# Up projection of a hybrid decoder layer: ten places for the split weights, and a small fp32 product per segment

## The chip, the core and the metric

The kernel runs on one core of one Trainium2 chip. The metric is the device time of one execution in microseconds; lower is better. The time before is 2170.84 us, the median of two runs (2167.92 and 2173.75).

## What is computed

One layer of a decoder on x of 512 tokens by 2048, in float32. Token mixing (a projection, gated linear attention in four heads, differential attention in four heads, an output projection) is followed by a gated MLP with a causal convolution over time. The change lies in the MLP's first product, `h @ w_ffn_in`:

```python
def conv_ffn(h, w_ffn_in, conv_w, conv_b, w_ffn_out):
    S = h.shape[1]
    up = h @ w_ffn_in
    a, b = up[..., :D_FF], up[..., D_FF:]
    a_pad = jnp.pad(a, ((0, 0), (CONV_W - 1, 0), (0, 0)))
    a = (conv_w[0] * a_pad[:, 0:S] + conv_w[1] * a_pad[:, 1:S + 1]
         + conv_w[2] * a_pad[:, 2:S + 2] + conv_b)
    return (jax.nn.gelu(a, approximate=True) * b) @ w_ffn_out
```

D_FF is 5632, so `w_ffn_in` has 2048 rows and 11264 columns, and `w_ffn_out` 5632 rows and 2048 columns.

## The kernel before

**Precision.** Every large product is made of three fp32r products: each operand is split into a high half (ScalarE rounds it to fp32r, line 135) and a low half (VectorE subtracts, line 136), and high x high, high x low and low x high are added up in PSUM. Products in plain fp32 (the small ones of attention, lines 439, 507, 538) are single calls of `mm`.

**Granules and the ring.** Weights come in granules of 128 x 1024 floats (512 KB). `granule` (line 126) splits one into two slots of a tile named ring, of 7 x 1024 columns (line 108). `halves` (line 111) takes the slots in turn: three for high halves (0, 1, 2) and three for low halves (3, 4, 5). `place_w` shifts every slot by so many columns of four bytes; the shift is the "place". Token operands lie in the tiles ah, al (high and low) and s5, s2, s3. Token operands, weights slots at place 0 and ring all begin at the same offset in a row of 128 columns (512 bytes), so place 16 sets weights 16 columns off the tokens.

**The up projection.** It begins with two pairs of column blocks by the plain scheme (`mm_t`, lines 163 to 173; place 0, lines 171 to 173), of which the first stands in a section whose order is written by hand (`to_ffn`). The other 40 blocks of 128 columns of each branch are made in ten groups `gi` of 4 blocks; each group has two units, one for each branch (`br`): 20 units in `ups` (line 1052). A unit is a Strassen-like scheme: seven segments x0, z0, y0, z1, x1, y1, y2 (lines 876 to 911) in place of eight block products. Each segment takes two granules of 24 matmuls (`up_prods`, lines 916 to 926: 128 x 128 weights, 256 tokens), so a unit has 7 x 2 x 24 = 336 matmuls. The order of segments is y0, z1, x1, y1 of a unit, x0 of the next, y2 of this, z0 of the next (lines 1053 to 1077). Some granules are sums of weight blocks: a DMA of GpSimd adds into the tile (line 873), or VectorE does (lines 889, 907). A unit's chains hold one PSUM bank each of two pools, psm (x and z) and psa (y), with four banks each.

**The down projection** (down units, lines 1015 to 1050, from line 1074 on) uses the same `run`, with 128 x 128 token blocks as weights and 512 columns of granule as the moving operand, at place 0. Its token operands are read back from DRAM and split (`prepare`, line 1010, with `split`, lines 147 to 149). The first down unit's x0 stands between y1 and y2 of the last up unit.

**What sets the order.** Outside the hand-written sections a scheduler orders each engine's instructions by a simulated timeline: an instruction that depends on nothing goes where the engine would otherwise wait. ScalarE, VectorE and TensorE then run their own lists in order, and semaphores carry the dependencies, those of overlapping columns of the ring among them.

Of the kernel before, what the change touches and what calls it, by code (L numbers as in the profile page):

```python
# [35 lines left out]
def hybrid_layer(ctx: ExitStack, tc: tile.TileContext, x, attn_pre_norm, w_in, w_alpha_up, b_alpha,  # L36
# [19 lines left out]
    mm = nc.tensor.matmul  # L56
# [5 lines left out]
    psa = ctx.enter_context(tc.tile_pool(name="psa", bufs=4, space=PSUM))  # L62


    ident = few.tile([P, P], F32, name="ident")
    make_identity(nc, ident)
    nhalf = few.tile([P, 4], F32, name="nhalf")
# [9 lines left out]
    def bank(pool=None):  # L77
        return (pool or psa).tile([P, 512], F32, name="bank", tag="bank")
# [27 lines left out]
    place_w = [0]  # L106
# [19 lines left out]
    def granule(src, a, raw=None, spare=None, hl=None):  # L126
        if raw is None:
            raw = load(src, a)
        if hl is not None:
            hi, lo = hl[:, 0, :], hl[:, 1, :]  # L130
        elif spare:
            hi, lo = spare_halves(spare)
        else:
            hi, lo = halves()
        act(hi, raw, AF.Copy)  # L135
        tt(lo, raw, hi.bitcast(F32), ALU.subtract)  # L136
        r = "p (a b) -> p a b"
        return hi.rearrange(r, a=a), lo.rearrange(r, a=a)
# [8 lines left out]
    def split(hi, lo, src):  # L147
        act(hi, src, AF.Copy)  # L148
        tt(lo, src, hi.bitcast(F32), ALU.subtract)  # L149
# [615 lines left out]
    def pair_tile():  # L765
        return small_tile("u").rearrange("p (n t) -> p n t", n=2)


    def conv(c, b, f):
        act(c, b, AF.Identity, bias=conv_col(3, f), scale=conv_col(2, f))  # L770
        stt(c[:, 1:], b[:, :S - 1], conv_col(1, f), c[:, 1:], ALU.mult, ALU.add)
        stt(c[:, 2:], b[:, :S - 2], conv_col(0, f), c[:, 2:], ALU.mult, ALU.add)
        act(c, c, AF.Gelu_apprx_tanh)
# [82 lines left out]
    class Unit:  # L856
# [4 lines left out]
        def run(self, seg, op, raws):  # L861
            c = seg[0]
            if seg[1] == "0":
                self.banks[c] = self.chain(c)
            for g in range(2):
                turn[0] += 1
                place_w[0] = 16 if self.a == 4 else 0
                hl = granule(None, self.a, raws[g], spare=extra[0] and turn[0] % 4 == 0)
                self.prods(self.banks[c], op, g, hl, seg[1] == "0")

# [42 lines left out]
    NOW = dict(skip_group_check=True)  # L913
# [16 lines left out]
    def up_unit(gi, br):  # L930
        col0 = DFF * br + 512 * gi
        T = [slice(0, 256), slice(256, 512)]
        st = {}

        def block(i, j, g):
            return w_f3[:, HK * i + 4 * g:HK * i + 4 * g + 4, col0 + 256 * j:col0 + 256 * (j + 1)]

        def chain(c):
            return bank(psa if c == "y" else psm)

        def out(seg, b):
            v = b.rearrange("p (n t) -> p n t", n=2)
            if seg == "x0":
                st["p1"] = fp.tile([P, 2, 256], F32, name="p1", tag="p1", bufs=2)
                act(st["p1"], v, AF.Copy)
            elif seg == "z0":
                st["u1"] = pair_tile()
                tt(st["u1"][:, :, T[1]], v, st["p1"], ALU.subtract)
            elif seg == "y0":
                stt(st["u1"][:, :, T[0]], v, -1.0, st["p1"], ALU.mult, ALU.subtract)  # L950
            elif seg == "z1":
                tt(st["u1"][:, :, T[0]], st["u1"][:, :, T[0]], v, ALU.add)
            elif seg == "x1":
                st["u0"] = pair_tile()
                act(st["u0"][:, :, T[0]], v, AF.Copy)
            elif seg == "y1":
                tt(st["u1"][:, :, T[1]], st["u1"][:, :, T[1]], v, ALU.subtract)
                if br == 0:
                    activate(1)
                else:  # L960
                    product(1)
            elif seg == "y2":
                tt(st["u0"][:, :, T[1]], v, st["p1"], ALU.add)
                if br == 0:
                    activate(0)
                else:
                    product(0)
                    token_sums(gi, st["u0"], st["u1"])

        def activate(j):  # L970
            c = held[gi, j] = pair_tile()
            for n in range(2):
                conv(c[:, n, :], st[f"u{j}"][:, n, :], 4 * gi + 2 * j + n)

        def product(j):
            u = st[f"u{j}"]
            tt(u, u, held.pop((gi, j)), ALU.mult)

        return Unit(4, block, up_prods, chain, out)


    def token_sums(gi, u0, u1):
        c, i = (gi - 1) // 2, (gi - 1) % 2
        T = [slice(0, 256), slice(256, 512)]
        a11, a21, a12, a22 = u0[:, :, T[0]], u0[:, :, T[1]], u1[:, :, T[0]], u1[:, :, T[1]]

        def put(n, src):
            dma(sd[c][n][:, i, :].rearrange("p (n t) -> p n t", n=2), src)

        def add(n, x, y, op):  # L990
            t = fp.tile([P, 2, 256], F32, name=n, tag="sum", bufs=2)
            tt(t, x, y, op)
            put(n, t)
            return t

        put("a11", a11)
        put("a12", a12)
        put("a22", a22)
        s5 = add("s5", a21, a22, ALU.subtract)
        s2 = add("s2", s5, a11, ALU.subtract)  # L1000
        add("s7", a11, a21, ALU.subtract)
        add("s3", s2, a12, ALU.add)
# [7 lines left out]
    def prepare(c, n):  # L1010
        raw = small_tile("st")
        dma(raw, sd[c][n].rearrange("p g x -> p (g x)"))
        split(piece(ah, *place[n]), piece(al, *place[n]), raw)
# [17 lines left out]
    def down_unit(c, cb):  # L1031
        def block(i, j, g):
            gi = 2 * c + 1 + g
            col = 1024 * cb + 512 * j
            return w_y3[:, 4 * gi + 2 * i:4 * gi + 2 * i + 2, col:col + 512]

        def chain(ch):
            return [bank(psm if ch == "x" else psa) for _ in range(2)]

        def out(seg, b):  # L1040
            for j in range(2):
                if seg == "x0":
                    into(accp[j][:, 512 * cb:512 * (cb + 1)], b[j], 1, c == 0)
                    continue
                half, col, sign = {"z0": (1, 1, 1), "y0": (0, 1, -1), "z1": (0, 1, 1), "x1": (0, 0, 1),
                                   "y1": (1, 1, -1), "y2": (1, 0, 1)}[seg]
                sl = slice(1024 * cb + 512 * col, 1024 * cb + 512 * (col + 1))
                into(acc[2 * half + j][:, sl], b[j], sign, c == 0 and seg in ("z0", "y0", "x1", "y2"))

        return Unit(2, block, down_prods, chain, out)  # L1050

    ups = [up_unit(gi, br) for gi in range(1, NG) for br in range(2)]
    for i, u in enumerate(ups):
        nxt = ups[i + 1] if i + 1 < len(ups) else None
        if i == 0:
            u.x0()
            u.z0()
        u.y0()
        u.z1()
        if i == 0:  # L1060
            for h, r in enumerate(s7raw):
                split(up["s7"][0][:, h], up["s7"][1][:, h], r)
        if nxt is None:
            prepare(0, "a11")
        u.x1()
        if nxt is None:
            prepare(0, "s5")
        u.y1()
        if nxt is not None:
            nxt.x0()  # L1070
            u.y2()
            nxt.z0()
        else:
            downs = [down_unit(c, cb) for c in range(NG // 2) for cb in range(2)]
            downs[0].x0()
            prepare(0, "s2")
            u.y2()
# [163 lines left out]
```

## Time and profile before

| what | us |
|---|---|
| median of two runs | 2170.84 |
| profiled execution: span from first to last instruction | 2150.8 |
| median less span | 20.0 |
| matmuls busy | 2112.4 |
| weight loads busy | 1875.4 |
| VectorE busy | 1414.6 |
| ScalarE busy | 898.3 |
| up projection in units, first to last matmul of lines 924 to 926 | 928 to 1705 |

The profile gives no device time of the profiled execution beside its span; it is set beside the median of the two runs. PE stands for matmuls and PEld for weight loads; both are issued by TensorE and overlap. A group's row names line, engine, operation, out<-in, shape and count, then busy us and mean ns of one, then idle time of the engine ahead of it and who ended it. In a timeline each row has start in us, length in us, engine, line and operation; in brackets the idle time before it and who ended that. Lengths of matmuls reach past the start of the next, so the pace of a stream is read from starts.

### The profile page before, as it was taken

How to read it: one execution, taken by the hardware profiler on the slowest of the kernel's cores; microseconds unless marked ns; L12 is line 12 of the kernel's file. 1: busy time of each engine (PE TensorE's matmuls, PEld its weight loads, DVE VectorE, ACT ScalarE, POOL GpSimd, SP SyncE). 2: the span in 40 equal slices, each digit the busy share in tenths (PEclk: the TensorE clock that was granted, in tenths of full speed). 3: DMA queues.
4: the chain of work that ended last, by engine and by line, in shares of the span. 5: the costliest groups of instructions: out<-in, count | busy, mean ns of one | idle time of the engine just before them, and what ended most of it. 6: DMA issues, size and time to landing. Idle time of an engine off the chain costs nothing.

```text
span 2150.8 us, 31861 instructions
## 1 busy us (share of the span) xinstructions
PE 2112.4 (98%) x13009; PEld 1875.4 (87%) x13009; DVE 1414.6 (66%) x1725; ACT 898.3 (42%) x1162; POOL 199.2 (9%) x242
## 2 busy tenths in 40 slices
PE   7999999999999999999999999999999899999998
PEld 6878888888888889999999999999999778787786
DVE  5345554443444237688777786777778777888887
ACT  4233332333343224344544553544454554443433
POOL 1000000000000001011111111111110111110100
PEclk9999999999999999999999999999999999999999
DMA  6322222223224335455776757667577777676653
GB/s 214 99 75 79 79 69 79 79 79 88 78 80 169 95 128 186 128 119 136 172 172 149 175 139 189 149 157 191 129 172 177 203 229 182 171 195 170 158 167 145
DMA packets 218471, 303.83 MB, mean 141 GB/s; under 512 B 11776, under 2 KB 155572, under 8 KB 216404
## 3 DMA queue, kind: packets, MB, share of 16 engines
q1 hardware_dynamic: 165204, 238.87, 33.4%
q0 software_dynamic: 53120, 62.92, 19.1%
q8 instruction: 102, 1.67, 0.3%
q14 instruction: 45, 0.37, 0.1%
HBM read 273.97 MB, written 27.79 MB: 140 GB/s over the span
## 4 chain that ended last, share of the span: by engine, by line
PE 46%; issue 45%; POOL 4%; DVE 3%; DMA 2%; ACT 1%; POOLq 0%; SPq 0%; DVEq 0%; ACTq 0%
PE bank L189 7%; PE bank L190 7%; PE bank L191 7%; PE bank L173 5%; PE bank L171 5%; PE bank L172 5%; POOL rt L873 2%; PE bank L926 2%; PE bank L925 2%; PE bank L924 2%; POOL raw L873 2%; PE bank L439 1%; PE bank L507 1%; PE bank L538 1%; DVE ring L136 1%
## 5 line engine op out<-in xcount | busy, mean ns | idle before, releaser
L136 DVE TENSOR_TENSOR ring<-raw,ring 128x1024 fp32r<-128x1024 f32 x305 | 371.6, 1221 | 353.8 <-ACT ring L135 344.1
L135 ACT ACTIVATE ring<-raw 128x1024 fp32r<-128x1024 f32 x305 | 323.1, 1060 | 596.6 <-PE bank L191 157.3
L926 PE MATMUL bank<-ah,ring 128*128 128x256 f32 x1280 | 353.7, 276 | 0.8 <-DVE ring L136 0.8
L924 PE MATMUL bank<-ah,ring 128*128 128x256 f32 x1280 | 353.5, 276 | 0.0
L925 PE MATMUL bank<-al,ring 128*128 128x256 f32 x1280 | 353.4, 276 | 0.0
L136 DVE TENSOR_TENSOR ring<-rt,ring 128x1024 fp32r<-128x1024 f32 x221 | 269.0, 1220 | 89.8 <-ACT ring L135 87.9
L135 ACT ACTIVATE ring<-rt 128x1024 fp32r<-128x1024 f32 x221 | 233.1, 1060 | 223.5 <-PE bank L925 146.1
L926 PEld LDWEIGHTS bank<-ah,ring 128*128 128x128 f32 x1280 | 240.3, 188 | 1.2 <-DVE ring L136 1.2
L925 PEld LDWEIGHTS bank<-al,ring 128*128 128x128 f32 x1280 | 240.4, 188 | 0.1
L924 PEld LDWEIGHTS bank<-ah,ring 128*128 128x128 f32 x1280 | 240.3, 188 | 0.1
L189 PE MATMUL bank<-ring,ah 128*128 128x512 f32 x600 | 236.9, 398 | 0.8 <-ACT ah L148 0.8
L190 PE MATMUL bank<-ring,ah 128*128 128x512 f32 x600 | 235.8, 394 | 0.0
L191 PE MATMUL bank<-ring,al 128*128 128x512 f32 x600 | 235.0, 394 | 0.0
L171 PE MATMUL bank<-ah,ring 128*128 128x512 f32 (+1 forms) x512 | 196.2, 383 | 0.0
L173 PE MATMUL bank<-ah,ring 128*128 128x512 f32 (+1 forms) x512 | 194.7, 380 | 0.0
L172 PE MATMUL bank<-al,ring 128*128 128x512 f32 (+1 forms) x512 | 194.5, 380 | 0.0
L1022 PE MATMUL bank<-ring,ah 128*128 128x512 f32 x424 | 166.7, 393 | 7.3 <-DVE ring L136 7.2
L1023 PE MATMUL bank<-ring,al 128*128 128x512 f32 x424 | 165.8, 391 | 0.0
L1021 PE MATMUL bank<-ring,ah 128*128 128x512 f32 x424 | 158.8, 393 | 3.2 <-ACT ring L135 2.4
L191 PEld LDWEIGHTS bank<-ring,al 128*128 128x128 f32 x600 | 113.2, 189 | 24.3 <-DVE al L149 0.3
L189 PEld LDWEIGHTS bank<-ring,ah 128*128 128x128 f32 x600 | 113.1, 189 | 24.2 <-ACT ah L148 1.2
L190 PEld LDWEIGHTS bank<-ring,ah 128*128 128x128 f32 x600 | 113.3, 189 | 23.7 <-DVE ring L136 0.5
(260 smaller groups left out, 4063.6 us busy)
## 6 DMA issues: line engine op xcount, KB each, us to landing
raw<-in_w_in_dram SPq DMA_DIRECT2D x96, 512.0 KB, 3.7
raw<-in_w_ffn_in_dram SPq DMA_DIRECT2D x96, 512.0 KB, 5.1
raw<-in_w_ffn_out_dram SPq DMA_DIRECT2D x48, 512.0 KB, 7.3
rt<-in_w_ffn_in_dram SPq DMA_DIRECT2D x40, 512.0 KB, 6.6
rt<-in_w_ffn_in_dram POOLq DMA_DIRECT2D x40, 512.0 KB, 6.2
raw<-in_w_ffn_in_dram POOLq DMA_DIRECT2D x40, 512.0 KB, 6.8
raw<-in_w_o_dram SPq DMA_DIRECT2D x32, 512.0 KB, 3.7
rt<-in_w_ffn_out_dram SPq DMA_DIRECT2D x20, 512.0 KB, 8.1
```

What stands on the lines that cost most here:

```text
L135: act(hi, raw, AF.Copy)
L136: tt(lo, raw, hi.bitcast(F32), ALU.subtract)
L171: mm(o, wh, ah[:, t0:t1, kk, :], start=st, stop=False)
L172: mm(o, wh, al[:, t0:t1, kk, :], start=False, stop=False)
L173: mm(o, wl, ah[:, t0:t1, kk, :], start=False, stop=sp)
L189: mm(banks[t], ah[:, t, s, :], w[0][:, k, :], start=st, stop=False)
L190: mm(banks[t], ah[:, t, s, :], w[1][:, k, :], start=False, stop=False)
L191: mm(banks[t], al[:, t, s, :], w[0][:, k, :], start=False, stop=sp)
L924: mm(o, wh, sh[:, :, kk, :], start=start and kk == 0 and n == 0, stop=False, **NOW)
L925: mm(o, wh, sl[:, :, kk, :], start=False, stop=False, **NOW)
L926: mm(o, wl, sh[:, :, kk, :], start=False, stop=kk == HK - 1, **NOW)
L1022: mm(b[j], sh[:, o:o + P], w[1][:, q, :], start=False, stop=False, **NOW)
```

## The change

```diff
             for g in range(2):
                 turn[0] += 1
-                place_w[0] = 16 if self.a == 4 else 0
+                place_w[0] = self.place if self.a == 4 else 0
+                if self.a == 4 and g == 0:
+                    mm(nudge[0][:, 0:4], ident, nhalf, start=True, stop=True, **NOW)
                 hl = granule(None, self.a, raws[g], spare=extra[0] and turn[0] % 4 == 0)
                 self.prods(self.banks[c], op, g, hl, seg[1] == "0")
...
+    nudge = [bank(psa)]
     ups = [up_unit(gi, br) for gi in range(1, NG) for br in range(2)]
+    for i, u in enumerate(ups):
+        u.place = (16, 32, 48, 64, 80, 96, 112, 8, 24, 0)[i // 2]
     for i, u in enumerate(ups):
         nxt = ups[i + 1] if i + 1 < len(ups) else None
```

Up units have `self.a == 4`, down units 2. The units of the first group keep place 16; the other nine groups get 32, 48, 64, 80, 96, 112, 8, 24 and 0, one place for each pair of units. Because x0 and z0 of the next unit stand around y2 of this one, the place changes three times where two groups meet. A product in plain fp32 (the identity, 128 x 128, as weights, four columns of -0.5 as the moving operand; line 869 of the changed kernel) is written at the first granule of each segment, 140 in all. It writes a PSUM bank of pool psa that nothing reads. In the changed kernel the lines behind line 866 move by 2, those behind line 1051 by 5.

## The prediction

> **What bounds the kernel now.** I read the page first (shares, then the costliest groups), then busy time by stretches, then the timeline of the stretch that the change touches.
>
> ```profile
> span 2150.8 us, 31861 instructions
> PE 2112.4 (98%) x13009; PEld 1875.4 (87%) x13009; DVE 1414.6 (66%) x1725; ACT 898.3 (42%) x1162; POOL 199.2 (9%) x242
> PEclk9999999999999999999999999999999999999999
> L136 DVE TENSOR_TENSOR ring<-raw,ring 128x1024 fp32r<-128x1024 f32 x305 | 371.6, 1221 | 353.8 <-ACT ring L135 344.1
> L135 ACT ACTIVATE ring<-raw 128x1024 fp32r<-128x1024 f32 x305 | 323.1, 1060 | 596.6 <-PE bank L191 157.3
> ```
>
> TensorE is busy for 98% of the span, so whatever lengthens its stream lengthens the kernel. The diff touches the up projection (matmuls of lines 924 to 926, from 928 to 1705 us). By stretches (columns: stretch, length, busy time and count of PE, PEld, DVE, ACT, POOL, clock, DMA):
>
> ```profile
> core 0: us, PE busy (x) PEld busy (x) DVE busy (x) ACT busy (x) POOL busy (x), PEclk, DMA share, GB/s
> 945.00:1130.00 185.00, 185.00 (x1635) 185.00 (x1634) 140.22 (x144) 89.45 (x99) 25.25 (x20) 1.00 0.70 163
> 1140.00:1340.00 200.00, 200.00 (x1767) 200.00 (x1766) 150.63 (x153) 91.66 (x99) 26.08 (x21) 1.00 0.72 171
> 1366.00:1569.00 203.00, 203.00 (x1793) 203.00 (x1792) 153.99 (x157) 92.53 (x101) 27.99 (x22) 1.00 0.71 167
> 1693.90:1697.00 3.10, 3.10 (x9) 2.45 (x8) 2.33 (x3) 1.18 (x2) 0.86 (x1) 0.51 0.79 159
> ```
>
> In the up projection matmuls and weight loads are both gapless: hundreds of us without a wait. DVE is at 75%, ACT under 50%, DMA at 70%. So the stage's time is the number of matmuls, 20 units of 336 = 6720, times the spacing of their starts. The whole list of waits holds only this for PE there (us in total, times, longest):
>
> ```profile
> PE bank L926 <- DVE ring L136: 1.8, 4, 0.6
> ```
>
> The spacing is not one number. First and last of 25, of 67 and of 64 matmuls, in that order, with the event ahead of them or behind them that matters (fp32 transposes at 837.77, waits at 943.40 and 1134.30):
>
> ```profile
> 837.77 1.15 PE L156 MATMUL bank<-ident,xr 128*128 128x128 f32 x9
> ...
> 839.11 0.28 PE L171 MATMUL bank<-ah,ring 128*128 128x256 f32 x1
> ...
> 841.98 0.28 PE L171 MATMUL bank<-ah,ring 128*128 128x256 f32 x1
> ```
> ```profile
> 928.03 0.28 PE L924 MATMUL bank<-ah,ring 128*128 128x256 f32 x1
> ...
> 935.80 0.28 PE L924 MATMUL bank<-s5h,ring 128*128 128x256 f32 x1
> ...
> 943.40 0.39 PE L926 MATMUL bank<-s2h,ring 128*128 128x256 f32 x1 [0.57 <-DVE ring L136]
> ```
> ```profile
> 1134.30 0.39 PE L926 MATMUL bank<-s2h,ring 128*128 128x256 f32 x1 [0.42 <-DVE ring L136]
> ...
> 1144.73 0.28 PE L924 MATMUL bank<-ah,ring 128*128 128x256 f32 x1
> ...
> 1151.87 0.28 PE L924 MATMUL bank<-ah,ring 128*128 128x256 f32 x1
> ```
>
> Line 171 multiplies the same shape from the ring at place 0: 2.87/24 = 0.120 us. The up projection at place 16 starts at 7.77/66 = 0.118 and later stands at 7.14/63 = 0.1133. So the same instruction has at least three paces; the first is at distance 0, the other two at distance 16. The 0.118 ends at the wait of 943.40 and does not come back: behind the wait of 1134.30 the pace is 0.1133 again.
>
> **The change, part by part.** *The products.* One fp32 product of 4 moving columns for each of 20 x 7 segments: 140. The nearest row is the fp32 product of line 439, 64 columns, which the trace shows as two instructions each (4 heads x 7 levels x 4 products = 112):
>
> ```profile
> L439 PE MATMUL bank<-qe,d 128*128 128x64 f32 x224 | 27.7, 268 | 0.0
> ```
> ```profile
> 160.72 0.39 PE L191 MATMUL bank<-ring,al 128*128 128x512 f32 x1
> 160.94 1.00 PE L439 MATMUL bank<-qe,d 128*128 128x64 f32 x8
> 161.75 0.48 PE L189 MATMUL bank<-ring,ah 128*128 128x512 f32 x1
> 162.07 1.00 PE L439 MATMUL bank<-qe,d 128*128 128x64 f32 x8
> 162.88 0.48 PE L190 MATMUL bank<-ring,ah 128*128 128x512 f32 x1
> 163.19 0.40 PE L191 MATMUL bank<-ring,al 128*128 128x512 f32 x1
> 163.43 0.40 PE L189 MATMUL bank<-ring,ah 128*128 128x512 f32 x1
> ```
>
> From 160.72 to 163.19 are 2.47 us for three 512-column matmuls (0.23 each by their undisturbed starts here, 0.22 to 0.24) and 16 fp32 instructions: 1.78/16 = 0.111 us each. Each instruction comes with a weight load of 128 columns, whatever it streams, so I take 0.111 for 4 columns too: 140 x 2 x 0.111 = **+31 us**. Lower end 0.81/8 = 0.101 from one batch alone (28 us), upper end 0.15 if each also ran dry, a third more than the row (42 us); I stay at the row. They are not at the heads of granules: nothing depends on them, and in the order of the built program they stand in 22 batches (of 1 to 15), all ahead of the middle of the group with place 80, where the scheduler saw PE wait. Four batches of 15 stand where the place goes back (below). The rest may swallow the four waits above: -1 us. Their PSUM bank is one of four of which the stage uses one at a time: nothing.
>
> *The places.* Each place holds for two units, 672 matmuls, so 1 ns of spacing is 0.67 us. Place 16 stays at 0.1133. Place 0 is line 171's case, 0.120: 672 x 6.7 ns = +4.5 us. For 64 the nearest rows are the forget gate's matmuls, whose weight slices are 80 columns wide, so that slice k begins 80k columns on:
>
> ```profile
> 124.77 0.40 PE L386 MATMUL bank<-ah,gas 128*80 128x512 f32 x1
> ...
> 126.60 0.40 PE L386 MATMUL bank<-ah,gas 128*80 128x512 f32 x1
> ...
> 128.44 0.40 PE L386 MATMUL bank<-ah,gas 128*80 128x512 f32 x1
> ```
>
> Of the 8 matmuls in each gap none but these has 0.40, and the pattern returns after 1.83 us, after four slices: 320 columns, 64 beyond two rows of 128. So distance 64 looks like distance 0, and 80 like 16: 64 costs +4.5 us, 80 nothing. For 32, 48, 96, 112, 8 and 24 no row exists; by the three paces they lie between 0.1133 (0) and 0.120 (+4.5 each). I take the middle, 0.1167: 6 x 672 x 3.3 ns = +13.4 us (0 to +27; a gain is not excluded, a 256-column stream could be faster).
>
> The Trainium skill speaks against any effect of distance: "TensorE: Matmul & The Clock Gate", section "Part 2: What happens when you issue a matmul", gives PE two independent SBUF read ports, so that a weight load takes nothing from a running matmul. By it this term would be 0. The trace's paces of 0.120 and 0.1133 for one shape do not agree, unless the way of entering alone makes them.
>
> *The ring where the place changes.* Slots are 1024 columns apart and shift with the place. Where a granule with a lower place follows one with a higher place, its first columns lie on the last ones of the granule just before, and its split must wait until PE is done with that. The kernel before has this once, at its end, where place 16 meets place 0:
>
> ```profile
> 1691.13 1.06 ACT L148 ACTIVATE ah<-st 128x1024 fp32r<-128x1024 f32 x1 [0.26 <-DMA st<-sd0s]
> 1705.81 1.06 ACT L135 ACTIVATE ring<-rt 128x1024 fp32r<-128x1024 f32 x1 [1.77 <-PE bank L925]
> ```
> ```profile
> 1693.33 0.50 PE L1022 MATMUL bank<-ring,ah 128*128 128x512 f32 x1 [4.65 <-DVE ring L136]
> ...
> 1706.92 0.73 PE L1021 MATMUL bank<-ring,ah 128*128 128x512 f32 x2 [1.03 <-ACT ring L135]
> 1708.35 0.50 PE L1022 MATMUL bank<-ring,ah 128*128 128x512 f32 x1 [0.69 <-DVE ring L136]
> ```
>
> At 1706.92 PE waits for the high half (ACT, 1.06), at 1708.35 for the low half (DVE, 1.22): 1.03 idle, and 1.43 from the one start to the other in place of the 0.45 of two matmuls: 2.0 us. In the changed program eleven such places lie in the stage. Four carry the batches of 15 products (15 x 0.222 = 3.3 us), which cover them. Seven lie behind the last batch (80 to 96, 96 to 112, twice each around 8 and 0, 8 to 24): by the slots three block both halves (2.0 us each), four the low half alone (about the DVE's 1.2). 3 x 2.0 + 4 x 1.2 = **+11 us** (5, if half of it is covered, to 18, if DVE's queue holds more work ahead). Behind the waiting ACT and DVE stand their evacuations; with DVE at 75% they catch up within a unit.
>
> At the end of the stage the last place is now 0, as in the down projection, so the waits above go: 4.65 + 1.03 + 0.69 = 6.4 us. The 4.65 came because the low half stood in DVE's queue behind a split that waited for a DMA (the L148 row); in the new order both low halves stand ahead of it. The stretch 1693.9 to 1697, in the table at the clock 0.51, loses another 1.5. Together **-8 us**. What is late next there is the split at 1691.13, needed only by z0, over 10 us later.
>
> Sum: 31.1 - 1 + 9.0 + 13.4 + 11 - 8 = +55.5 us, on the profiled span of 2150.8: 2206. The median of the two runs, 2170.84, is 20 us above that span, so 2226 us, 2.6% more.
>
> **The rivals.** (A) Distance does nothing: the 0.120 is of another way of entering, and all ten places run at 0.1133 as each stall or product kicks them there. Then both place terms vanish: 31.1 - 1 + 11 - 8 = +33, 2204 us, 1.5% more, within 2%. For it: one place, 16, shows two paces. Against: line 171 enters its 0.120 behind fp32 transposes (837.77), just such a kick. It decides when the eight other places average below about 0.1152. The skill's rule of two ports, above, is this rival.
>
> (B) Other distances beat 16: the six unknown ones stand near 0.109 (the transposes of 837.77, of another shape: nine starts in 0.90 us, so PE can hold 0.100). Then 6 x 672 x -4.3 ns = -17 in place of +13: 2196 us. No row of this shape shows it; 0.1133, held over the 1635 matmuls of the first stretch, looks like a floor.
>
> (C) The products do not do what is said of them: behind place 80 no product stands, a group entered from a flowing stream stays at 0.118 or 0.120 (as at 928 us), and 120 becomes the rule: the six at +27 in place of +13, 16 and 80 half the time at 0.118 (672 x 4.7 ns = +3): 2243 us.
>
> (D) Clock: 15 tiny products keep the array nearly idle for 3.3 us. The trace shows half the clock behind an idle 4.65 us, for the 3.1 us of that row. Four batches, each followed by 3.1 us at half the clock, cost 4 x 1.55 = +6: 2232 us. The fp32 batches of line 439 (0.8 us) show no such thing, but are short. The skill's page named above, section "Part 1: The HAM clock gate", has the clock fall to half after one idle window of about 3.4 us; the trace's 4.65 us agrees, and no run here shows a batch of 3.3.
>
> **How the numbers follow.** Forecast 0.40 (own range 2214 to 2240), A 0.22, B 0.08, C 0.18, D 0.12. A measurement of this kernel can tell about 2% (43 us, 2214) from no change. C, D and nine tenths of the forecast lie above, with a small part of A: slower 0.68; faster needs -43 where even B ends above: 0.02; same 0.30. The range leaves out half of B and the far end of C and D: 2200 to 2246.
>
> **What would show it.** The spacing of the up projection's matmuls in ten groups: 0.120 at places 0 and 64, 0.1133 at 16 and 80, something between elsewhere. Line 869: 280 instructions, 0.111 apart. PE waits of 1 to 2 us on ACT or DVE at the last five changes of place, none of 4.65 at the stage's end. Wrong if the products cost far less than 0.2 us each, if a place runs below 0.113 or above 0.121, or if 64 and 0 differ.

## The result and the profile after

| | us |
|---|---|
| before, two runs beside the changed kernel | 2170.84 (2167.92 to 2173.75) |
| after, two runs | 2224.31 (2223.70 to 2224.92) |
| ratio | 1.0254, 95% interval 1.0224 to 1.0285 |
| profiled execution after: time, span | 2224.92, 2223.2 |

Ratios and their intervals, here and below, are estimates from the faster executions of both kernels, so they are not the quotients of the medians beside them (here 1.0246).

The kernel became 2.5% slower, by 53.5 us. The spans, however, are 72.4 us apart (2150.8 and 2223.2), and in the profiled execution after only 1.7 us lie outside the span. So the profiled execution of the kernel before was no 2170 us execution with 20 us around it, as the prediction took it. It was a shorter one: the kernel before has two paces in its up projection, an execution can hold either or change from one to the other, and most of its times fall into two groups (first experiment). Where that matters below, it is said which pace a run had.

The page of the changed kernel, the rows that answer to those shown of before:

```profile
span 2223.2 us, 32446 instructions
PE 2183.2 (98%) x13289; PEld 1948.1 (88%) x13289; DVE 1419.5 (64%) x1725; ACT 901.8 (41%) x1162; POOL 199.1 (9%) x242
...
L136 DVE TENSOR_TENSOR ring<-raw,ring 128x1024 fp32r<-128x1024 f32 x305 | 372.2, 1223 | 355.8 <-ACT ring L135 351.2
...
L928 PE MATMUL bank<-ah,ring 128*128 128x256 f32 x1280 | 363.8, 284 | 5.3 <-DVE ring L136 5.3
```

TensorE has 280 instructions more (13289 for 13009), 70.8 us more of busy time, and still 98%. DVE and ACT have what they had. All of the loss is in TensorE's own stream and its waits. From the first matmul of the up projection's units to the first one of the down projection behind the last of them are 854.2 us (928.73 to 1782.89) for 778.9 before (928.03 to 1706.92): 75.3 more, and the rest of the kernel 2.9 less.

The pace by place. Stretches of the changed kernel in which one place runs without a product or a wait: 80, 96, 112, 8, 24, 0. The length divided by the count is the spacing, once 2.4 is taken off the count for matmuls that were already running at the left edge (0.28 us long, 0.118 apart):

```profile
1310.00:1350.00 40.00, 40.00 (x355) 40.00 (x354) 30.27 (x32) 21.68 (x25) 5.08 (x4) 1.00 0.67 157
1372.00:1430.00 58.00, 58.00 (x491) 58.00 (x490) 45.36 (x48) 27.83 (x31) 7.64 (x6) 1.00 0.65 150
1454.00:1515.00 61.00, 61.00 (x521) 61.00 (x520) 46.78 (x49) 29.59 (x33) 7.63 (x6) 1.00 0.65 153
1538.00:1595.00 57.00, 57.00 (x483) 56.99 (x483) 43.66 (x46) 27.95 (x31) 7.66 (x6) 1.00 0.63 148
1620.00:1675.00 55.00, 55.00 (x466) 55.00 (x465) 43.12 (x46) 26.39 (x29) 7.62 (x6) 1.00 0.66 151
1705.00:1770.00 65.00, 65.00 (x545) 65.00 (x543) 48.78 (x51) 31.65 (x35) 8.83 (x7) 1.00 0.68 172
```

The first is 40/352.6 = 0.1134, the second 58/488.6 = 0.1187, the last 65/542.6 = 0.1198. Taken from the starts of all matmuls of a place (distances under 0.2 us), in ns, and the excess over 113.33 for its 672 matmuls, in us:

| place | 16 | 32 | 48 | 64 | 80 | 96 | 112 | 8 | 24 | 0 |
|---|---|---|---|---|---|---|---|---|---|---|
| ns | 116.28 | 118.66 | 117.91 | 120.00 | 114.63 | 118.64 | 117.78 | 118.43 | 118.47 | 119.96 |
| us | 2.0 | 3.5 | 3.1 | 4.4 | 0.9 | 3.5 | 3.0 | 3.4 | 3.4 | 4.4 |

At 16 and 80 these are means over two paces, 113.33 and 117.78, each held for dozens to hundreds of matmuls.

A batch of 15 products (30 instructions) and what stands behind it:

```profile
1010.82 3.41 PE L869 MATMUL bank<-nhalf,ident 128*128 128x4 f32 x30
1014.09 0.36 PE L926 MATMUL bank<-ah,ring 128*128 128x256 f32 x1
...
1016.45 0.41 PE L926 MATMUL bank<-ah,ring 128*128 128x256 f32 x1
1016.66 0.41 PE L927 MATMUL bank<-al,ring 128*128 128x256 f32 x1
...
1021.57 0.28 PE L926 MATMUL bank<-ah,ring 128*128 128x256 f32 x1
```

The 30 instructions take 3.27 us from first to next start, 0.109 each. From 1016.45 to 1021.57 a matmul takes 0.213 us: half the clock. Matmuls at this distance stand behind three of the four batches of 15, for 5.1, 3.2 and 5.3 us; two matmuls behind each of these three come five products more. The clock's own column (ahead of the DMA share) shows that half the clock begins earlier than those matmuls, and in the third batch (at 1275.30) within the batch itself:

```profile
1014.80:1021.50 6.70, 6.70 (x33) 6.70 (x33) 2.45 (x2) 0.86 (x1) 0.00 (x0) 0.50 0.21 71
1277.60:1287.70 10.10, 10.10 (x48) 10.10 (x49) 2.54 (x3) 1.06 (x1) 0.00 (x0) 0.50 0.23 72
```

So some products were slowed as well: the 30 instructions of the third batch take 4.18 us, and the five products behind the first and third 1.68 and 1.99 us, where five take 1.03 elsewhere. The fourth batch, at 1101.58, is not followed by half the clock (why: e11). Half the clock also stands behind the waits at 1684.83 and 1686.97 below (1687.2 to 1690.6).

The waits at the changes of place behind place 80, rows of three of the seven:

```profile
1364.08 0.39 PE L928 MATMUL bank<-ah,ring 128*128 128x256 f32 x1 [0.96 <-DVE ring L136]
...
1444.81 0.39 PE L926 MATMUL bank<-ah,ring 128*128 128x256 f32 x1 [1.03 <-ACT ring L135]
1446.07 0.39 PE L928 MATMUL bank<-ah,ring 128*128 128x256 f32 x1 [0.76 <-DVE ring L136]
...
1684.83 0.38 PE L926 MATMUL bank<-ah,ring 128*128 128x256 f32 x1 [1.03 <-ACT ring L135]
1686.97 0.43 PE L928 MATMUL bank<-ah,ring 128*128 128x256 f32 x1 [1.64 <-DVE ring L136]
```

The first blocks the low half alone, the other two both halves. At the stage's end the 4.65 us of before is gone, but waits stay in place of those of 1.03 and 0.69, though no place falls there any more. Ahead of the half that PE waits for, ACT has a split that waits for a DMA (first row; the half itself begins at 1781.79):

```profile
1779.40 1.06 ACT L148 ACTIVATE ah<-st 128x1024 fp32r<-128x1024 f32 x1 [3.55 <-DMA st<-sd0s]
...
1782.89 0.73 PE L1023 MATMUL bank<-ring,ah 128*128 128x512 f32 x2 [0.79 <-ACT ring L135]
1784.22 0.50 PE L1024 MATMUL bank<-ring,ah 128*128 128x512 f32 x1 [0.60 <-DVE ring L136]
```

### The profile page after: what moved, and what is told of

The parts are those of the page before. It is cut to its first block, busy times and chain, and to the rows that moved or that the text cites. A ratio compares the mean times of both kernels' runs of the same rounds, so it can differ in the third digit from the quotient of the medians.

```text
span 2223.2 us, 32446 instructions
## 1 busy us (share of the span) xinstructions
PE 2183.2 (98%) x13289; PEld 1948.1 (88%) x13289; DVE 1419.5 (64%) x1725; ACT 901.8 (41%) x1162; POOL 199.1 (9%) x242
## 4 chain that ended last, share of the span: by engine, by line
PE 81%; issue 13%; DVE 2%; DMA 1%; POOL 1%; ACT 1%; SPq 0%; POOLq 0%; DVEq 0%; ACTq 0%
PE bank L928 12%; PE bank L926 12%; PE bank L927 12%; PE bank L189 6%; PE bank L190 6%; PE bank L191 6%; PE bank L173 5%; PE bank L171 5%; PE bank L172 5%; PE bank L869 1%; PE bank L439 1%; PE bank L1024 1%; PE bank L1023 1%; PE bank L1025 1%; DVE ring L136 1%
## 5 line engine op out<-in xcount | busy, mean ns | idle before, releaser
L928 PE MATMUL bank<-ah,ring 128*128 128x256 f32 x1280 | 363.8, 284 | 5.3 <-DVE ring L136 5.3
L926 PE MATMUL bank<-ah,ring 128*128 128x256 f32 x1280 | 363.5, 284 | 2.1 <-ACT ring L135 2.1
L927 PE MATMUL bank<-al,ring 128*128 128x256 f32 x1280 | 362.9, 283 | 0.0
L928 PEld LDWEIGHTS bank<-ah,ring 128*128 128x128 f32 x1280 | 245.9, 192 | 6.3 <-DVE ring L136 6.3
L926 PEld LDWEIGHTS bank<-ah,ring 128*128 128x128 f32 x1280 | 245.8, 192 | 2.5 <-ACT ring L135 2.5
L927 PEld LDWEIGHTS bank<-al,ring 128*128 128x128 f32 x1280 | 245.8, 192 | 0.1
L190 PEld LDWEIGHTS bank<-ring,ah 128*128 128x128 f32 x600 | 113.4, 189 | 23.7 <-DVE ring L136 0.5
```

The lines of the kernel that those rows point to most:

```text
L190: mm(banks[t], ah[:, t, s, :], w[1][:, k, :], start=False, stop=False)
L926: mm(o, wh, sh[:, :, kk, :], start=start and kk == 0 and n == 0, stop=False, **NOW)
L927: mm(o, wh, sl[:, :, kk, :], start=False, stop=False, **NOW)
L928: mm(o, wl, sh[:, :, kk, :], start=False, stop=kk == HK - 1, **NOW)
```

## The experiments

Theory: the loss is the sum of the prediction's terms (products, pace by distance, waits at changes of place). Rivals: the distance matters little and the products are nearly all of it (A); the products or the batches do something of their own to pace or clock (C, D). "Pace" is the distance from one matmul's start to the next within the up projection, from all starts, unless a row is shown.

**The kernel before once more (e1_again).** No edit.

> The kernel before, unchanged. Theory (distance and entry): at distance 16 two paces are stable, 0.1133 and 0.1178 us, and each execution lands in one or the other behind each wait; so its times scatter between about 2150 (all fast, as in the profile shown) and 2182 us (all slow: 6720 x 4.45 ns more), and the span of the new profile is 2150.8 plus 4.45 ns for each further matmul at 0.1178. Rival (the scatter lies elsewhere): the up projection stays at 0.1133 throughout and other stages differ.

2149.69 us (2145.13 to 2169.50, 10 runs), beside 2166.70 (2140.60 to 2175.52, 19 runs) of the same kernel: 0.9989, interval 0.9945 to 1.0034. Of those 19, seven lie at 2140.6 to 2150.8 and twelve at 2162.6 to 2175.5; of the ten, two lie between (2158.0 and 2160.1). The profiled execution belongs to the lower group:

```profile
930.00:941.00 11.00, 11.00 (x96) 11.00 (x95) 11.00 (x12) 5.68 (x6) 0.00 (x0) 1.00 0.22 63
950.00:1650.00 700.00, 700.00 (x6178) 700.00 (x6178) 538.76 (x549) 338.23 (x369) 94.13 (x74) 1.00 0.69 164
```

It enters the stage at 0.1178; a wait at 942 (0.33 us from start to start) ends that, and the other 6500 matmuls run at 700/6175.6 = 0.1133. With the slow pace they would take 6500 x 4.45 ns = 29 us more, which is about the distance of the two groups (some 25 us). No execution of this kernel from the upper group was profiled. That the pace is what sets the groups apart is borne out by later experiments at two-pace places: the profile of e10 held the slow pace, that of e4 changed over in the midst of the stage, and both kernels' times spread alike.

**The ten places without products (e2_places).**

```diff
-                place_w[0] = 16 if self.a == 4 else 0
+                place_w[0] = self.place if self.a == 4 else 0
...
+    for i, u in enumerate(ups):
+        u.place = (16, 32, 48, 64, 80, 96, 112, 8, 24, 0)[i // 2]
```

> The ten places without the fp32 products. Theory: paces by distance modulo 64 columns as in the changed kernel: 0.120 at 0 and 64, 0.1187 at 32 and 96, 0.1178 at 48 and 112, 0.1184 at 8, 0.117 to 0.119 at 24, 0.1133 or 0.1178 at 16 and 80; eleven waits at changes of place, each 1.2 us or 1.3 + 1.0; no half clock in the up projection but where two waits stand close together; 2185 to 2197 us. Rival A (distance does nothing): all ten groups at 0.1133 or 0.1178 by luck, 2165 to 2190 us, and groups 0 and 64 not at 0.120.

2201.45 us (2197.49 to 2205.72, 4 runs), above the 2185 to 2197 expected; 1.0255, interval 1.0220 to 1.0289 against the kernel before beside it. That is the ratio of the whole change, but the two stand beside different executions of the kernel before. By spans, against the same 2150.8, the places alone (2195.8) cost 45.0 of the 72.4 us. In the stage (827.9 us, 49.0 more than before) pace makes +31, waits some +18, distances at half the clock +6.4, the stage's end some -7. All eleven changes of place now show PE waiting, most for 1.2 to 1.3 us from start to start (2.05 at the last), and after some where both halves wait PE runs at half the clock (why only some: e11):

```profile
1008.00:1011.00 3.00, 3.00 (x16) 3.00 (x15) 2.45 (x2) 0.41 (x1) 0.00 (x0) 0.50 0.75 211
```

Rival A falls: distance sets the pace. Only 16 showed 113.33 for most of its matmuls, from a wait at 942 on; 80 had 117.78 and, at its two ends, 113.4.

**The products without the places (e3_products).** All groups at place 16, the 140 products as in the change.

> The 140 products without the places (place 16 for all). Theory: 280 instructions at 0.111 us, +31 us over the kernel before in the same state; the pace behind a batch is 0.1133 or 0.1178 by chance, so 2184 to 2213 us. Rival (the products are kicks that put the stream into the fast pace): nearly all at 0.1133, 2184 us. Half the clock wherever a batch of 15 or more stands.

2192.95 us (2190.81 to 2193.84, 4 runs), 1.0213, interval 1.0187 to 1.0240. By spans the products alone (2191.2) cost 40.4 us against 2150.8. With no stall at the changes of place to fill, the scheduler now puts most products one by one. From one such product to the next but one (48 matmuls in each interval):

```profile
1256.88 0.28 PE L869 MATMUL bank<-nhalf,ident 128*128 128x4 f32 x2
1257.01 0.36 PE L926 MATMUL bank<-s5h,ring 128*128 128x256 f32 x1
1257.21 0.28 PE L927 MATMUL bank<-s5l,ring 128*128 128x256 f32 x1
...
1262.75 0.28 PE L869 MATMUL bank<-nhalf,ident 128*128 128x4 f32 x2
...
1268.44 0.28 PE L869 MATMUL bank<-nhalf,ident 128*128 128x4 f32 x2
```

The same number of matmuls takes 5.87 and then 5.69 us: the pace goes 117.78, 113.33, 117.78 and so on, changed by each of 57 single products and each of 19 groups of three, five or nine (eight of the threes are one and then two, with two matmuls between); two groups of four keep it. In this execution about half the matmuls stand at each pace. If the others did the same, that explains why the four times scatter by 3 us in place of 30. A product that stands alone delays the matmul behind its successor too: 1256.76 to 1257.21, 0.45 to 0.47 us for what two matmuls do in 0.236. That is 0.23 us a product.

**One place, 48 (e4_place48).** `16 if self.a == 4` becomes `48 if self.a == 4`.

> The kernel before with place 48 in place of 16, nothing else. Theory: only the pace 0.1178 exists there, so the span is 2150.8 + 6500 x 4.45 ns = 2180 us, time about 2181, and the runs scatter by less than those of the kernel before. Rival A: no difference from the kernel before, 2165 to 2175 us with its scatter.

2171.76 us (2143.63 to 2174.59, 10 runs), 1.0065, interval 1.0014 to 1.0115. It has the same two paces, not 117.78 alone as expected from e2 and the changed kernel; the profiled execution changed from one to the other at a wait (0.48 us from start to start):

```profile
945.00:1105.00 160.00, 160.00 (x1415) 160.00 (x1414) 122.83 (x126) 76.57 (x83) 22.34 (x18) 1.00 0.69 159
1120.00:1680.00 560.00, 560.00 (x4757) 560.00 (x4756) 419.56 (x426) 260.93 (x284) 71.23 (x56) 1.00 0.67 159
```

160/1412.6 = 0.1133, then 560/4754.6 = 0.1178.

**Does a product toggle the pace? (e5_toggle)** Place 16, and products tied to a granule so that they stand at the head of x1: 1, 2, 1, 2, 3 of them in units 3, 6, 9, 12, 15.

```diff
                 hl = granule(None, self.a, raws[g], spare=extra[0] and turn[0] % 4 == 0)
+                if self.a == 4 and g == 0 and seg == "x1":
+                    for _ in range(self.kicks):
+                        mm(nudge[0][:, 0:4], ident, hl[0][:, 0, 0:4].bitcast(F32), start=True, stop=True, **NOW)
```

> The kernel before at place 16 with fp32 products tied to the first granule of segment x1 (so that they stand at its head): one in unit 3, two in unit 6, one in unit 9, two in unit 12, three in unit 15. Theory (a product turns the stream from one pace to the other): the pace changes between 0.1133 and 0.1178 at units 3, 9 and 15 and stays at units 6 and 12; some +2 us for the products. Rival (the products are kicks to the fast pace, or to a random one): no such parity; behind every product 0.1133, or either by luck.

2167.50 us, one run. The stretches between the five places:

```profile
945.00:1060.00 115.00, 115.00 (x1018) 115.00 (x1017) 89.71 (x93) 58.40 (x65) 15.39 (x13) 1.00 0.67 154
1064.00:1182.00 118.00, 118.00 (x1004) 118.00 (x1003) 87.06 (x89) 52.58 (x56) 15.26 (x12) 1.00 0.67 160
1186.00:1298.00 112.00, 112.00 (x953) 112.00 (x952) 86.02 (x88) 55.97 (x63) 14.29 (x12) 1.00 0.62 150
1302.00:1420.00 118.00, 118.00 (x1004) 118.00 (x1003) 87.11 (x88) 52.67 (x56) 15.28 (x12) 1.00 0.66 159
1424.00:1532.00 108.00, 108.00 (x956) 108.00 (x955) 85.33 (x89) 55.34 (x62) 13.97 (x11) 1.00 0.64 155
1536.00:1700.00 164.00, 164.00 (x1395) 164.00 (x1394) 121.92 (x125) 76.72 (x83) 20.36 (x16) 1.00 0.69 164
```

Fast, slow, slow, slow, fast, slow. One product changed the pace once and once did not; two kept it once and changed it once; three changed it. So the rule that e3 suggests, an odd number of products changes the pace and an even number keeps it, does not hold in general: it failed here at 1300 (one, kept) and 1422 (two, changed). The products here differ from those of e3 in their moving operand (four columns of the granule). They also do not all stand alike: the scheduler put the single ones (with the first two matmuls of x1 behind them) and the three in the middle of z1, and the pairs where x1 begins.

**Ten other distances (e6_other_places), and ten close to 16 and 48 (e9_near_places).** As e2, with 4, 12, 20, 28, 36, 40, 44, 52, 56, 60 and then 14, 15, 17, 18, 46, 47, 49, 50, 54, 58.

> Ten other distances, without the products: 4, 12, 20, 28, 36, 40, 44, 52, 56, 60. Theory: each distance has one or two paces of its own between 0.113 and 0.121; 40 and 56 like 8 and 24 shifted (0.117 to 0.1187); total 2185 to 2205 us with the waits at the changes. Rival: a distance exists with one pace at or below 0.1133, which would be seen as a whole group without 0.117 or more.

> The kernel before with ten other distances for the groups of the up projection: 14, 15, 17, 18, 46, 47, 49, 50, 54, 58 columns; no added product. If the pace is set by the distance as a smooth function with a floor at 16 and 48 (theory), the neighbours stand between 0.1133 and 0.1178, with 17 and 49 next to 16, and 54 and 58 near the 0.1167 of 52 and 56. If there is a distance with one pace only, at or below 0.1135, it shows here. Rival: 16 and 48 are special because they are multiples of 16 columns (64 bytes); then 15, 17, 47 and 49 jump to 0.118 to 0.120, all alike. Time 2160 to 2200, not the point of this run.

2198.91 and 2200.99 us, one run each. Paces in ns:

| place | 4 | 12 | 20 | 28 | 36 | 40 | 44 | 52 | 56 | 60 |
|---|---|---|---|---|---|---|---|---|---|---|
| ns | 118.33 | 118.34 | 118.66 | 119.99 | 119.98 | 119.99 | 118.10 | 116.67 | 116.67 | 117.33 |

| place | 14 | 15 | 17 | 18 | 46 | 47 | 49 | 50 | 54 | 58 |
|---|---|---|---|---|---|---|---|---|---|---|
| ns | 117.79 | 119.51 | 118.33 | 118.34 | 117.78 | 118.34 | 117.78 | 117.78 | 119.99 | 117.78 |

Places 15, 17 and 50 of the second, as three rows of its stretches:

```profile
1018.00:1084.00 66.00, 66.00 (x555) 66.00 (x554) 48.98 (x51) 30.89 (x34) 8.57 (x7) 1.00 0.63 148
1099.00:1165.00 66.00, 66.00 (x560) 66.00 (x559) 49.37 (x53) 31.32 (x35) 8.69 (x7) 1.00 0.62 148
...
1509.00:1575.00 66.00, 66.00 (x563) 66.00 (x562) 49.78 (x52) 31.62 (x35) 8.59 (x7) 1.00 0.62 148
```

Both expectations failed in part: 40 (119.99) and 56 (116.67) are not like 8 and 24, 54 (119.99) is not like 52, and 15, 17, 47 and 49 are neither next to 113.33 nor all alike. No distance here comes to 113.33, and none beats it. One column aside of 16 the pace is 118.33 or 119.51, so no smooth dip at 16 shows. In the runs of this case 113.33 was seen at 16, 48 and 80 only, and there only part of the time. But each distance was held here by one group of one execution, and five of them (14, 46, 49, 50, 58) stood at 117.78 or 117.79, the slower pace of 16 and 48. Place 48 too had shown 117.78 alone in e2, and then 113.33 in e4. So a second, faster pace at some of these distances is not excluded.

**One place, 0 (e7_place0).** `16` becomes `0`.

> The kernel before with place 0 in place of 16. Theory: one pace, 0.120, so 6600 x 6.7 ns = +44 us over the fast state of the kernel before (2149) and -8 us because no place changes at the end of the stage: 2185 us, with a scatter of less than 10 us. Rival A (distance does nothing): 2149 to 2175 us as before.

2183.85 us (2183.09 to 2185.33, 4 runs), 1.0119, interval 1.0023 to 1.0215. 6671 matmuls in one run at 120.00 ns, without a wait up to the stage's end, and a scatter of 2 us:

```profile
950.00:1690.00 740.00, 740.00 (x6169) 740.00 (x6168) 541.91 (x548) 338.12 (x368) 94.13 (x74) 1.00 0.66 155
```

**Place 16 in every stage (e8_place16_all).** Place 16 also for the other stages, the down projection among them.

> Place 16 in every stage, the 512-column products included. Theory: where the ring gives the weights (plain up blocks, projections by lines 171 to 173) the pace falls from 0.2267 by up to 7 ns (1344 matmuls, -9 us) and from 0.120 to 0.1133 or 0.1178 in the 256-column ones; where the ring is the moving operand distance 16 stands with the other sign and may be worse; the waits at the stage's end go (-8 us). 2135 to 2175 us. Rival: the 512-column products keep 0.2267, only the waits go.

2177.70 us (2151.34 to 2184.35, 10 runs), above the 2135 to 2175 expected; 1.0079, interval 1.0030 to 1.0128. The matmuls of 512 columns went from 0.227 us apart to 0.233 where the ring gives the weights (lines 171 to 173) and to 0.229 to 0.230 where it is the moving operand (lines 189 to 191 and 1021 to 1023; means of three lines): what is good for one shape is bad for the other.

**A place that only rises (e10_rising).** 128 in place of 0 from the first granule of the down projection on.

```diff
-                place_w[0] = 16 if self.a == 4 else 0
+                place_w[0] = 128 if self.a == 2 or place_w[0] == 128 else 16
```

> The kernel before, except that from the first granule of the down projection on the place is 128 in place of 0 (the same distance in a row of 128 columns), also for the last segment of the up projection that stands behind it. A slot then never begins below where the slot before it ended. If the waits at the stage's end come from a place that falls from 16 to 0 (theory), the waits of 4.65, 1.03 and 0.69 us there and the stretch at half the clock are all gone: about 8 us, the time about 8 below the kernel before at the same pace of the stream. Rival: the 4.65 is DVE's queue behind the split that waits for a DMA (line 148), whatever the places; then a wait of 3 to 5 us stays and the gain is 2 to 3. The 512-column products should keep their spacing (128 and 0 are the same distance); if they go from 0.227 to 0.230 or more, as they did at place 16, the time rises by 10 and more instead.

2163.04 us (2140.12 to 2169.12, 10 runs), 0.9986, interval 0.9935 to 1.0037: within the spread that the two paces make. The profiled execution ran at the slow pace and shows the stage's end:

```profile
1723.65 1.06 ACT L148 ACTIVATE ah<-st 128x1024 fp32r<-128x1024 f32 x1 [4.84 <-DMA st<-sd0s]
...
1727.14 0.73 PE L1021 MATMUL bank<-ring,ah 128*128 128x512 f32 x2 [2.20 <-ACT ring L135]
1728.48 0.50 PE L1022 MATMUL bank<-ring,ah 128*128 128x512 f32 x1 [0.61 <-DVE ring L136]
```

The wait of 4.65 and the half clock are gone. A wait of 2.20 for the high half took the place of the 1.03 one: on ACT the split that waits for a DMA (1723.65) now stands ahead of the half that PE waits for. Some 5 us are won in the trace (2.20 and 0.61 for 4.65, 1.03, 0.69 and 1.5 at half the clock), of the 8 expected. So both causes seem to have been at work, the falling place and the queue behind the DMA; each kernel has one profile of this spot.

**Batches of products at a steady pace (e11_batches), and all products there (e12_place0_products).** Both at place 0, where the pace is one. The first has 15, 15, 12, 10, 5 and 20 products at the first granule of x1 in six units (made as in e5), where no place changes. The scheduler put three of the first 15, of the 12, of the 5 and of the 20 half a segment earlier, so that batches of 12, 15, 9, 10, 2 and 17 stand where x1 begins. The second has the 140 of the change.

> Place 0 in the whole up projection (one pace, 120.00 ns, no waits) and batches of the four-column fp32 product behind one another: 12, 15, 9, 10 and 17 of them, 2.7, 3.3, 2.0, 2.2 and 3.8 us long by 0.222 each, at the heads of five segments, where no place changes. If the batch itself lets the clock fall (rival D of the prediction), the matmuls behind 15 and 17 stand 0.213 us apart for some 3 us, those behind 9 and 10 do not, and 12 may go either way. Rival: the half clock behind the batches of 15 in the changed kernel came of the change of place beside them; then no batch here is followed by it.

> Place 0 in the whole up projection, and the 140 products as in the changed kernel, where the scheduler puts them one by one. At one pace the price of the products stands alone: 0.222 for each, and a longer start of the matmul behind each group, as seen at place 16 (465 ns from the matmul ahead of a product that stands alone to the second behind it, 229 more than two matmuls): about 32 us over the 2183.85 of place 0 without them, so 2216. If the products also change the pace at distance 0, as they did at distance 16, it shows as two paces, and the time is lower than 2210.

The first: 2209.49 us, one run. Behind 15, 10 and 17 products (3.3, 2.15 and 3.7 us) and from within the 12 on (2.9 us, the end of it already slowed) stand 3.41 us each at half the clock, behind 9 (1.93 us) none. The clock (the column ahead of the DMA share) behind 15 and behind 9:

```profile
1200.90:1203.50 2.60, 2.60 (x14) 2.60 (x14) 0.00 (x0) 0.00 (x0) 0.00 (x0) 0.50 1.04 376
1325.80:1328.00 2.20, 2.20 (x21) 2.20 (x20) 0.17 (x1) 0.00 (x0) 0.00 (x0) 1.00 0.45 133
```

So it is the batch, not the change of place beside it. The expectation for 10 products failed: 2.15 us suffice. The drop comes late: that batch ends at 1448.70, the half clock begins at 1449.70. The granted clock shows why. Within a run it changes only on a grid of 3.41 us: in the changed kernel the half clock begins at 1014.74, 1192.23, 1277.56 and 1687.16, which lie 52, 25 and 120 times 3.41 us apart, and lasts 6.83, 3.41, 10.24 and 3.41. What counts, then, is how much of one such window is without large matmuls, be it by waits or by small products. Added up for every window at the full clock, in the up projections of all runs and the 30 us behind them (0.120 us counted for each 256-column matmul, 0.225 for each 512-column one), the result is sharp: the 29 windows with 2.08 us or more were each followed by half the clock; none with 2.05 or less was. The batch of 9 and a little beside it make 2.01, the batch of 10 makes 2.23. The fourth batch of the changed kernel (at 1101.58) is cut by a window's edge into 1.91 and 1.45. Of the pairs of waits in e2, one whose window holds 2.31 us of them (at 1004.76) was followed by half the clock, and one that an edge cuts (at 1415.17; 1.75 us in the fuller window) was not.

The Trainium skill ("TensorE: Matmul & The Clock Gate", section "Part 1: The HAM clock gate") asks for an idle window of about 3.4 us. The length agrees with the 3.41 us here. But the window need not be idle throughout: 2.15 us of four-column products in it were followed by half the clock, and the measurement decides.

The second: 2215.06 us (2214.10 and 2216.03), 31.2 us over place 0 without products, as expected. Distance 0 keeps its 120.00 throughout; there the products cost their own time, the late starts behind them among it, and nothing else.

## Why the prediction was right, and where it was wrong

The measured 2224.31 us lies 2 us from the forecast of 2226, but that closeness is luck: two errors of 17 and 18 us cancelled. The terms themselves held in the main. The sum was 16.9 us short on the span (55.5 for 72.4), and the 20 us added for what lies around the span are in truth 1.7. By its terms, from the starts of all matmuls of the stage (products run from the start of a group to that of the matmul behind it, waits are distances over 0.225 us, the clock's term those from 0.2 to 0.225; the borders between rows are good to some 0.5 us):

| term, us | predicted | measured |
|---|---|---|
| products | +31.1 | +30.7 |
| pace of the ten places | +22.4 | +30.4 |
| waits: seven changes of place, less those of before | +10 | +10.8 |
| half the clock, late starts behind products | 0 | +9.9 |
| the stage's end | -8 | -6.6 |
| the rest of the kernel | 0 | -2.9 |

- *Products: right.* The batches of 15 took 0.109 us an instruction, as the row of line 439 had it (0.111), though they stream 4 columns in place of 64. The 30.7 is for the 134 products in the stage; six stand ahead of it. Some 2.5 of it are products at half the clock. Missed was the late start of the matmul behind a group (0.20 in place of 0.118), 2.3 us of the clock's row. With the one and without the other a product cost 0.228 us, for the 0.222 of the sum.
- *Places 0 and 64: right,* 8.8 us for 9.0. Reading the modulus of 64 columns from the 80-column slices of line 386 held.
- *The six unknown places: mis-sized.* Taken at the middle, 0.1167 (+13.4), they measured 0.1178 to 0.1187 (+19.9), inside the bounds of 0 to 27 that were kept. They lie nearer the slow end: of 30 distances measured only 16, 48 and 80 showed 113.33 at all (e6, e9).
- *16 and 80: wrong.* "Place 16 stays at 0.1133" and "80 nothing" assumed that 0.1133, once reached, stays. 16 and 80 have two paces, and the products and waits of the change moved the stream between them: +2.9 us.
- *Waits: right in place and in size.* All seven uncovered changes showed, three with both halves, four with one; those of 1683 and 1699 took 1.9 instead of 1.2 for the low half.
- *Clock: the step left out.* The sum had no clock term, rival D had. Three of the four batches of 15 were followed by half the clock, and so was one pair of waits: 80 matmuls at 0.213, 80 x 0.100 = 8 us, and the 2.5 us of slowed products, for D's 6. D took the 3.1 us of its row as the length of the half clock; that is the length of the stretch asked for, and the half clock there lasts 3.41 (1693.96 to 1697.37).
- *The stage's end: in part wrong.* That "the waits above go" held for the 4.65 us and the half clock. The waits of 1.03 and 0.69 came back as 0.79 and 0.60 behind a split that waits for a DMA, which the sum had at nothing.
- *The 20 us around the span: wrong.* The step was "The median of the two runs, 2170.84, is 20 us above that span". Times are 1.7 us above spans here (2224.92 and 2223.2); the rest was the other pace. Against an execution at the fast pace (2149, e1) the change costs 75 us, against one at the slow pace (2175) 49.

Rival A fell by e2, and with it what the prediction drew from the rule of the Trainium skill ("TensorE: Matmul & The Clock Gate", "Part 2: What happens when you issue a matmul"), that two independent read ports make distance free: e7 at place 0 measures 120.00 in place of 113.33 or 117.78 with nothing else changed. B fell by the changed kernel, where the six stood at 117.78 and above, and no distance of e6 and e9 came below 113.33. C was half right: 16 and 80 did spend time at 117.78, for a reason it did not have; the six stood below 0.120.

Open: what chooses between the two paces. Waits of PE of 0.21, 0.40 and 0.48 us (from start to start) were followed by the slow one, of 0.33, 0.37 and 0.85 by the fast one, and four of 0.31 to 0.70 in the kernel before left the fast one as it was. A version that always stays at the fast pace, 2140 to 2150 us by the lower group, would beat the kernel before, but no run here found how to hold it there; e10 gains 5 us in its trace and nothing that the times can tell. Why the distance matters is open too, and so is whether it is the distance: for the 256-column matmuls only the weights were moved, so their own place in the row is a rival that no run here parts from it. (For 512 columns e8 moved the moving operand of lines 1021 to 1023 alone, and their pace changed, 0.227 to 0.230.)

## What to carry to other kernels

Before a change is costed against a profile, see which of its kernel's times the profiled execution belongs to: a median beside a span of another pace put 18 us into this forecast. A stream of matmuls with a new weight load each has a pace that hangs on how far weights and moving operand stand apart, for each shape anew, and moving the one by a single column can cost up to 5% (113.33 to 119.51 ns here); measure the distance that is used, more than once, and do not interpolate. Filler products are paid in full when the stream is gapless, 0.22 us each here, and where they and the waits fill more than some 2 us of one 3.41 us window they cost the clock as well.

## What the runs showed of the hardware

- The spacing of fp32r matmuls of 256 columns with a weight load each takes values from 113.33 to 120.00 ns by the distance of the operands in columns; 0 and 64, 16 and 80, 32 and 96, 48 and 112 go together.
- At 16, 48 and 80 the same stream holds one of two paces, 113.33 or 117.78 ns, over thousands of matmuls. A wait or a small fp32 product can move it from one to the other. Distance 0 showed one pace only (e7, e11, e12).
- A product of four columns in plain fp32 is two instructions of 0.109 us in a batch of 15; with 64 columns it is two of 0.111.
- The granted clock changes only on a grid of 3.41 us, and a window of it with 2.08 us or more of waits and small products was followed by half the clock for the next 3.41 us at least; one with 2.05 us or less was not. So 2.15 us of products were enough, and 3.3 us were not where a window's edge cut them in two.
